# Low parts of six weight granules per layer subtracted on GpSimd instead of VectorE

## The chip, the cores and the metric

The kernel runs on one core of a Trainium2 chip. The core's engines are TensorE (PE in the profile, its weight loads PEld), VectorE (DVE), ScalarE (ACT), GpSimd (POOL) and SyncE (SP, which here only issues DMAs). Each engine works through its own instructions in order, and engines wait for one another by semaphores. The metric is the device time of one execution in microseconds. Before the change the median of three runs is 723.58 us (723.31 to 723.88).

## The reference

The program is a decoder trunk of two layers for 256 tokens of width 1024, in float32. Each layer projects x with w_in into the queries, keys and values of two attention branches and two gates, runs a stick-breaking attention and a block-sparse softmax attention, merges the branches, and adds a SwiGLU part with its own norm:

```python
branch_sb = merge_heads(o_sb) @ w_branch_sb
branch_mb = merge_heads(o_mb) @ w_branch_moba
merged = jax.nn.sigmoid(g_sb) * branch_sb + jax.nn.sigmoid(g_mb) * branch_mb
mix = merged @ w_out
x = layer_norm(DEEPNORM_ALPHA * x + mix, ...)
x = layer_norm(DEEPNORM_ALPHA * x + swiglu(x, w_gate, w_up, w_down), ...)
```

## The kernel before

**Weights.** All weights of a layer come as 122 granules of 128 x 1024 float32 (512 KB each). A product in float32 is made of three matmuls on rounded values (the type fp32r): with a = a_hi + a_lo for both sides, it is hi x hi, hi x lo and lo x hi (`mm3`). So each granule needs two parts. `WeightStream.line` makes them: SP loads the granule into one of six `raw` buffers; ACT casts it to the high part (`whi<-raw`, a ring of ten slots); then DVE subtracts, `wlo = raw - whi` (`wlo<-raw,whi`, a second ring of ten). Both operands of this subtraction lie in SBUF. The load of granule g + 6 waits until granule g has been subtracted, because it reuses its buffer. Seven granules per layer (`SOFT_IN_LAYER`, 22 to 40) take another way: POOL issues two DMAs that cast and accumulate, without DVE.

**The stage that matters here.** Within a layer, granules 40 to 47 are the two branch projections (40 to 43 the stick-breaking one, whose results are called pa, 44 to 47 the MoBA one, pb), and 48 to 55 the output projection (pw), one granule for each 128 rows of w_out. In the profile and in the built program layer 1's granules are 122 higher: 45 is 167 there. While TensorE works on pa, the MoBA heads come to an end (pp and mb_w: the parts of their weights; mb_o: their products; mb_f and mb_turn: their sums; omb_hi and omb_lo: the parts of their result). Then TensorE works on pb, which reads omb. DVE multiplies the gates with pa and pb (each product with one operand in PSUM, where matmuls write), adds the two gates of a chunk (`l0gate<-l0gate`, both operands in one SBUF tile), and ACT and DVE make the parts m_hi and m_lo, which TensorE reads in pw. After pw comes the norm, whose two small steps `ve` run on POOL.

**The order.** The code fixes the order of each engine's instructions while it is built. `Weave` keeps an estimated clock for each engine (`act_t`, `dve_t`, `pool_t`, and `t` for TensorE). Side works such as `line` are generators; after each group of three matmuls `tick` runs those that are due by the estimated clocks. When an estimate changes, instructions change places on all engines. `dve` counts n/960 us and a fixed part for an instruction, `act` n/1200, and `pool` 0.55 us for whatever it is given.

Of the kernel before, what the change touches and what calls it, by code (L numbers as in the profile page):

```python
# [7 lines left out]
F32 = mybir.dt.float32  # L8
# [21 lines left out]
GCOLS = 1024  # L30
NG_LAYER = 122
# [3 lines left out]
class Weave:  # L35
# [18 lines left out]
        self.dve_t = max(self.dve_t, e) + n / 960.0 + DVE_FIXED  # L54
        return self.dve_t + HOP

    def pool(self, e, f, *args, **kw):
        f(*args, **kw)
        self.pool_t = max(self.pool_t, e) + 0.55
        return self.pool_t + HOP  # L60

    def add(self, gen, due=0.0, last=False):
# [36 lines left out]
class WeightStream:  # L99
# [5 lines left out]
    def __init__(self, nc, pool, rings, w, total, weave):  # L105
        self.nc, self.pool, self.rings, self.w, self.total, self.weave = nc, pool, rings, w, total, weave
        self.soft = [g for g in range(total) if SOFT(g)]
        self.hard = [g for g in range(total) if not SOFT(g)]
        self.loaded = self.split = self.cast = self.done = 0
        self.limit = NSPLIT - 1  # L110
        self.current = 0
        self.dma_t = 1.7
        self.raw, self.parts, self.there, self.ready = {}, {}, {}, {}
# [36 lines left out]
    def _part(self, i, g):  # L150


        at = g % NSPLIT * GCOLS + (ON[i] if self._on(g) else 0)
        return self.rings[i][:, at:at + GCOLS]
# [4 lines left out]
    def line(self):  # L159

        nc, weave = self.nc, self.weave
        while self.split < len(self.hard):
            g = self.hard[self.split]
            ahead = g - self.current
            if g > self.limit:
                yield weave.t + 0.1
                continue
            if ahead >= LEAD and max(weave.dve_t, weave.act_t) > weave.t + BACKLOG:
                yield weave.t + 0.2
                continue  # L170
            self.load(self.split + NRAW)
            if ahead > 0:
                yield self.there[g]
            hi, lo = (self._part(i, g) for i in range(2))
            t = self.raw.pop(g)
            e = weave.act(self.there[g], GCOLS, nc.scalar.copy, hi, t)
            if g - self.current > 0:
                yield e
            e = weave.dve(e, GCOLS, nc.vector.tensor_sub, lo, t, hi.bitcast(F32))
            self.parts[g], self.ready[g] = (hi, lo), e  # L180
            self.split += 1
            self.load(self.split + NRAW)
# [36 lines left out]
    def allow(self, g):  # L219

        reaches = self._on(g) and not self._on(g - NSPLIT + 1) and g % NSPLIT < NSPLIT - 1
        self.limit = max(self.limit, min(g - reaches, self.total - 1))
# [25 lines left out]
    return g % NG_LAYER in SOFT_IN_LAYER  # L248


NSPLIT = 10
ON = (16, 48)
STATIONARY = ((8, 20), (24, 50), (64, 100), (130, 140), (146, 170), (186, 220))
# [15 lines left out]
def hybrid_trunk_kernel(ctx: ExitStack, tc: tile.TileContext, w, xT_in, x_in, ln_in,  # L269
# [39 lines left out]
    def turn(e):  # L309

        was = None
        while True:
# [5 lines left out]
            else:  # L318
# [3 lines left out]
        return taken[0] - 1  # L322
    rings = [p.tile([P, NSPLIT * GCOLS + on], F32R, name=n)
             for p, n, on in ((ring0, "whi", ON[0]), (ring1, "wlo", ON[1]))]
# [137 lines left out]
    def both_tokens(name, g0, put):  # L462

        acc = [bankM(f"{name}{t}", [P, WIDTH]) for t in range(2)]
        for t, k in ((0, 0), (0, 1), (0, 2), (1, 0), (1, 1), (0, 3), (1, 2), (1, 3)):
            tok_major(acc[t], g0 + k, t, k == 0, k == 3, 2 * k)
            if t == 1:
                ws.allow(g0 + k + NSPLIT)
            if k == 3:
                put(t, acc[t])  # L470

    def first_projections(names, puts):

        acc = [bankB(n, [P, 2, WIDTH]) for n in names]
        for kc in range(KC):
            for j in range(2):
# [7 lines left out]
                if kc % 2:  # L484
                    ws.allow(g + NSPLIT)
                if kc == KC - 1:
# [245 lines left out]
    def two_pairs(line, name, ps, qks, free, e, sides, *args):  # L732


        while len(turned) < free:
            yield
        e = max(e, *turned[max(free - 2, 0):free], 0.0)
        yield e + MARGIN
        ss = [bankB(f"{name}{p}_s", [P, 2, 512]) for p in ps]
        pe_after(e)  # L740
        e = scores([(s, *qk) for s, qk in zip(ss, qks)])
        for p, s in zip(ps, ss):
            sides.append(weave.add(line(f"{name}{p}", p, s, e, *args)))
# [17 lines left out]
    def norm_line(name, t, junk, gb):  # L761

        x = xs[t]
        st = small.tile([P, 2], F32, tag="st", name=f"{name}_st{t}")
        nmu = small.tile([P, 1], F32, tag="nmu", name=f"{name}_nmu{t}")
        ve = small.tile([P, 1], F32, tag="ve", name=f"{name}_ve{t}")
        e = pe_done()
        for h in range(2):
            e = residual(e, x, halves[h], junk[:, h, :], st[:, h:h + 1])
        e = dve(e, 16, nc.vector.tensor_scalar, nmu, st[:, 0:1], st[:, 1:2], -1.0 / D, op0=OP.add, op1=OP.mult)  # L770
        e2 = act(e, D + 100, nc.scalar.activation, junk, x.rearrange("p (h c) -> p h c", h=2), AF.Square,
                 bias=nmu, accum_out=ve)
        e2 = pool(e2, nc.gpsimd.tensor_scalar, ve, ve, 1.0 / D, EPS, op0=OP.mult, op1=OP.add)
        e2 = pool(e2, nc.gpsimd.tensor_tensor, ve, ve, mhalf, op=OP.pow)
        ends = [e for _, e in scale_shift(e, x, halves, nmu, OP.add, ve, *gb, e2)]
        for h in range(2):
            i = yield from turn(ends[h])
            tp = bankC(f"{name}_tp{t}{h}", [P, 4, P])
            pe_after(ends[h])
            for j in range(4):  # L780
                transpose(tp[:, j, :], x[:, (4 * h + j) * P:(4 * h + j + 1) * P])
            ks = slice(h * 4, (h + 1) * 4)
            ts = slice(t * P, (t + 1) * P)
            e = pe_done()
            yield e
            left[i] = xT_ready[t] = yield from split_line(xT_hi[:, ks, ts], xT_lo[:, ks, ts], tp, 512, e)
# [33 lines left out]
    for l in range(DEPTH):  # L820
# [41 lines left out]
        def sb_pair(p, g):  # L862
            hi, lo = (pl.tile([P, 2, S], F32R, tag=f"qk{n}{p % 2}", name=f"{L}qk{n}{p}", bufs=1)
                      for n, pl in (("hi", work), ("lo", page2 if p % 2 else work)))
            ps = bankM(f"{L}pqk{p}", [P, 2, S])
            feat_major(ps[:, 0, :], g)
            feat_major(ps[:, 1, :], g + 1)
            qks[p] = [(hi[:, i, :], lo[:, i, :]) for i in range(2)]

            def line():  # L870
                ends[p] = yield from split_line(hi, lo, ps, 512, pe_done())
                if p % 2:
                    e = max(ends[p - 1], ends[p])
                    yield e + MARGIN
                    yield from two_pairs(sb_line, f"{L}sb", (p - 1, p), (qks[p - 1], qks[p]),
                                         l * 2 * NPAIR + p - 1, e, sides, v_sb, o_sb, sigmoids, passed)

            sides.append(weave.start(line()))
# [280 lines left out]
```

## Time and profile before

| | us |
|---|---|
| median of three runs | 723.58 |
| the profiled execution, its own time | 723.1 |
| its span, first to last instruction | 721.3 |
| TensorE busy | 710.4 |
| DVE busy | 526.5 |
| ACT busy | 389.7 |
| POOL busy | 34.5 |

The span is what the trace covers; the execution's own time has 1.8 us around it. A row of the timeline reads: start, duration, engine, line, operation, output <- inputs, shapes, count; in brackets the idle time before it and what ended that. Several instructions of one kind in a row are merged (x4), with the whole duration. Buffer numbers are left out there. An instruction's duration is a little longer than its distance to the next, since successive instructions overlap slightly.

### The profile page before, as it was taken

To read this page: it belongs to the slowest core of one execution; us is meant where nothing else is said; L and a number is where in the kernel's file an instruction comes from. 1 tells how busy PE (TensorE), PEld (TensorE's weight loads), DVE (VectorE), ACT (ScalarE), POOL (GpSimd) and SP (SyncE) were. 2 spreads that over 40 slices of the span, in tenths; PEclk is the share of its full clock that TensorE was granted. 3 is DMA by queue.
4 is the path that set the end of the run, shared out by engine and by line. 5 is a ranking of instruction groups with operands and counts; after the bars stand their busy time and mean duration, and the time that the engine had idled before them with its cause. 6 is when DMAs were issued, how large, how long until landed. Compare 5 with 4: busy or idle time off the path is not lost.

```text
span 721.3 us, 12733 instructions
## 1 busy us (share of the span) xinstructions
PE 710.4 (98%) x4992; PEld 651.9 (90%) x4992; DVE 526.5 (73%) x786; ACT 389.7 (54%) x581; POOL 34.5 (5%) x48
## 2 busy tenths in 40 slices
PE   9999999999999999999999999999999999999995
PEld 7889899987899999988889889999888999998885
DVE  5999886798886666644588887869989776665416
ACT  5767667663665554533356566776556555454300
POOL 0001110000000000000000111000010000000001
PEclk9999999999999999999999999999999999999998
DMA  8998889677596656476259579695748965562501
GB/s 287 343 337 238 232 209 267 208 273 239 183 330 224 200 184 202 146 290 205 65 176 354 158 215 233 199 307 177 271 164 290 292 201 184 198 202 93 229 1 59
DMA packets 61597, 156.26 MB, mean 217 GB/s; under 512 B 10720, under 2 KB 21984, under 8 KB 61536
## 3 DMA queue, kind: packets, MB, share of 16 engines
q1 hardware_dynamic: 56848, 140.50, 57.6%
q0 software_dynamic: 4544, 14.68, 9.2%
q8 instruction: 39, 0.64, 0.4%
q10 hardware_dynamic: 144, 0.26, 0.1%
q14 instruction: 22, 0.18, 0.1%
HBM read 148.08 MB, written 7.34 MB: 215 GB/s over the span
## 4 chain that ended last, share of the span: by engine, by line
PE 92%; DVE 3%; DMA 3%; ACT 1%; issue 0%; POOL 0%; SPq 0%; POOLq 0%; DVEq 0%; ACTq 0%
PE l1pf L427 14%; PE l0pf L427 14%; PE l0pd L427 8%; PE l0pg L427 6%; PE l1pg L427 6%; PE l1pe L427 4%; PE l1pd L427 4%; PE l1pqk L427 3%; PE l1pw L427 3%; PE l1pft L427 3%; PE l0pft L427 3%; PE l1pvq L427 3%; PE l0pw L427 2%; DMA raw<-in_w_dram 2%; PE l0pv L427 2%; PE l1pk L427 2%
## 5 line engine op out<-in xcount | busy, mean ns | idle before, releaser
L53 DVE TENSOR_TENSOR wlo<-raw,whi 128x1024 fp32r<-128x1024 f32 (+1 forms) x234 | 277.2, 1202 | 81.2 <-ACT whi L48 78.3
L48 ACT CAST whi<-raw 128x1024 fp32r<-128x1024 f32 (+1 forms) x233 | 237.6, 1036 | 81.7 <-PE l0pd L427 19.6
L427 PE MATMUL l1pf<-xT_hi,wlo 128*128 128x256 f32 x288 | 79.6, 276 | 0.0
L427 PE MATMUL l1pf<-xT_hi,whi 128*128 128x256 f32 x288 | 79.6, 276 | 0.0
L427 PE MATMUL l1pf<-xT_lo,whi 128*128 128x256 f32 x288 | 79.6, 276 | 0.0
L427 PE MATMUL l0pf<-xT_hi,whi 128*128 128x256 f32 x288 | 79.5, 276 | 0.0
L427 PE MATMUL l0pf<-xT_hi,wlo 128*128 128x256 f32 x288 | 79.5, 276 | 0.0
L427 PE MATMUL l0pf<-xT_lo,whi 128*128 128x256 f32 x288 | 79.5, 276 | 0.0
L427 PEld LDWEIGHTS l1pf<-xT_lo,whi 128*128 128x128 f32 x288 | 54.1, 188 | 0.0
L427 PEld LDWEIGHTS l1pf<-xT_hi,whi 128*128 128x128 f32 x288 | 54.1, 188 | 0.0
L427 PEld LDWEIGHTS l1pf<-xT_hi,wlo 128*128 128x128 f32 x288 | 54.1, 188 | 0.0
L427 PEld LDWEIGHTS l0pf<-xT_hi,whi 128*128 128x128 f32 x288 | 54.1, 188 | 0.0
L427 PEld LDWEIGHTS l0pf<-xT_lo,whi 128*128 128x128 f32 x288 | 54.1, 188 | 0.0
L427 PEld LDWEIGHTS l0pf<-xT_hi,wlo 128*128 128x128 f32 x288 | 54.1, 188 | 0.0
L427 PE MATMUL l0pg<-xT_hi,whi 128*128 128x256 f32 x128 | 35.8, 280 | 0.2 <-DVE l0vmb L53 0.2
L427 PE MATMUL l1pg<-xT_hi,whi 128*128 128x256 f32 x128 | 35.7, 279 | 0.0
L427 PE MATMUL l0pg<-xT_hi,wlo 128*128 128x256 f32 x128 | 35.4, 277 | 0.0
L427 PE MATMUL l0pg<-xT_lo,whi 128*128 128x256 f32 x128 | 35.4, 277 | 0.0
L427 PE MATMUL l1pg<-xT_lo,whi 128*128 128x256 f32 x128 | 35.4, 276 | 0.0
L427 PE MATMUL l1pg<-xT_hi,wlo 128*128 128x256 f32 x128 | 35.3, 276 | 0.0
L427 PE MATMUL l0pd<-whi,l0h_hi 128*128 128x512 f32 x88 | 34.5, 392 | 0.0
L427 PE MATMUL l0pd<-whi,l0h_lo 128*128 128x512 f32 x88 | 34.3, 389 | 0.0
(365 smaller groups left out, 1783.9 us busy)
## 6 DMA issues: line engine op xcount, KB each, us to landing
raw<-in_w_dram SPq DMA_DIRECT2D x226, 512.0 KB, 4.7
whi<-in_w_dram POOLq DMA_DIRECT2D x14, 512.0 KB, 5.1
wlo<-in_w_dram POOLq DMA_DIRECT2D x14, 512.0 KB, 6.4
ln<-in_ln_dram SPq DMA_DIRECT2D x8, 512.0 KB, 6.1
raw<-in_w_dram SPq DMA_DIRECT2D x7, 256.0 KB, 5.7
l0mb_scr<-l0mb_turn SPq DMA_DIRECT2D x4, 384.0 KB, 5.0
l0mb_turn<-l0mb_scr SPq DMA_DIRECT2D x16, 96.0 KB, 6.2
l1mb_scr<-l1mb_turn SPq DMA_DIRECT2D x4, 384.0 KB, 7.3
```

Source lines behind the costliest of these rows:

```text
L48: f(*args, **kw)
L53: f(*args, **kw)
L427: nc.tensor.matmul(o, a, b, start=start, stop=stop)
```

## The change

Six granules of each layer, 45, 47, 49, 51, 53 and 55 counted within the layer, get their low part by GpSimd's `tensor_sub` in place of VectorE's. `pool` gets an argument for the time to count, and these six count 2.4 us on POOL's estimated clock. Operands, result and what waits for it are otherwise the same.

```diff
-    def pool(self, e, f, *args, **kw):
+    def pool(self, e, f, *args, took=0.55, **kw):
         f(*args, **kw)
-        self.pool_t = max(self.pool_t, e) + 0.55
+        self.pool_t = max(self.pool_t, e) + took
         return self.pool_t + HOP
...
-            e = weave.dve(e, GCOLS, nc.vector.tensor_sub, lo, t, hi.bitcast(F32))
+            if g % NG_LAYER in POOLED:
+                e = weave.pool(e, nc.gpsimd.tensor_sub, lo, t, hi.bitcast(F32), took=POOL_SUB)
+            else:
+                e = weave.dve(e, GCOLS, nc.vector.tensor_sub, lo, t, hi.bitcast(F32))
...
+POOLED = (45, 47, 49, 51, 53, 55)
+POOL_SUB = 2.4
```

Since the order follows the estimated clocks, other instructions of the stage move as well. On DVE in layer 0, while TensorE works on pa, there stood before (the number behind raw is the granule):

```order
L53 TENSOR_TENSOR wlo_99<-raw45_1442,whi_98 128x1024
L53 TENSOR_TENSOR l0gate1_1129<-l0gate1_1129,l0pa1_1644 128x2x256
L53 TENSOR_TENSOR pp_168<-l0mb2_turn_1375,pp_168 128x768
L53 TENSOR_TENSOR l0omb_lo_1018<-l0mb1_f_1630,l0omb_hi_1017 128x256
L53 TENSOR_TENSOR l0gate2_1310<-l0gate2_1310,l0pa2_1678 128x2x256
L53 TENSOR_TENSOR l0mb3_w1_1704<-l0mb3_turn_1412,l0mb3_w0_1703 128x768
L53 TENSOR_TENSOR wlo_99<-raw46_1477,whi_98 128x1024
```

and now:

```order
L53 TENSOR_TENSOR l0gate1_1129<-l0gate1_1129,l0pa1_1644 128x2x256
L53 TENSOR_TENSOR pp_168<-l0mb2_turn_1375,pp_168 128x768
L53 TENSOR_TENSOR wlo_99<-raw46_1477,whi_98 128x1024
L53 TENSOR_TENSOR l0omb_lo_1018<-l0mb1_f_1630,l0omb_hi_1017 128x256
L53 TENSOR_TENSOR l0mb3_w1_1714<-l0mb3_turn_1412,l0mb3_w0_1713 128x768
L53 TENSOR_TENSOR l0gate2_1310<-l0gate2_1310,l0pa2_1679 128x2x256
L53 TENSOR_TENSOR wlo_99<-raw48_1504,whi_98 128x1024
```

Granule 45 has left DVE, 46 has moved ahead of omb_lo and of mb3_w1 (mb_w in the profile), and the product with pa2 behind it. On TensorE the matmuls that read mb3_w come six matmuls earlier in layer 0 and twelve later in layer 1.

On DVE in layer 0, while TensorE begins pw, before:

```order
L53 TENSOR_TENSOR wlo_99<-raw51_1665,whi_98 128x1024
L53 TENSOR_TENSOR l0gate3_1455<-l0gate3_1455,l0pb3_1768 128x2x256
L53 TENSOR_TENSOR l0m1_lo_1846<-l0gate2_1310,l0m1_hi_1845 128x512
L53 TENSOR_TENSOR l0gate3_1455<-l0gate3_1455 128x2x256
L53 TENSOR_TENSOR wlo_99<-raw52_1729,whi_98 128x1024
L53 TENSOR_TENSOR wlo_99<-raw53_1789,whi_98 128x1024
L53 TENSOR_TENSOR wlo_99<-raw54_1807,whi_98 128x1024
L53 TENSOR_TENSOR wlo_99<-raw55_1824,whi_98 128x1024
L53 TENSOR_TENSOR l0m1_lo_1846<-l0gate3_1455,l0m1_hi_1845 128x512
```

and now:

```order
L53 TENSOR_TENSOR l0gate3_1455<-l0gate3_1455,l0pb3_1778 128x2x256
L53 TENSOR_TENSOR l0m1_lo_1846<-l0gate2_1310,l0m1_hi_1845 128x512
L53 TENSOR_TENSOR l0gate3_1455<-l0gate3_1455 128x2x256
L53 TENSOR_TENSOR wlo_99<-raw54_1756,whi_98 128x1024
L53 TENSOR_TENSOR l0m1_lo_1846<-l0gate3_1455,l0m1_hi_1845 128x512
```

One subtraction of four is left ahead of the last m_lo, that of granule 54; granule 52 stands further up, ahead of the first m_lo.

On POOL in layer 0, between the last weight DMA and the norm, there is now:

```order
L134 DMA wlo_99<-in_w_dram 128x2x512
L58 ISA
L58 TENSOR_TENSOR wlo_99<-raw45_1442,whi_98 128x1024
L58 TENSOR_TENSOR wlo_99<-raw47_1491,whi_98 128x1024
L58 TENSOR_TENSOR wlo_99<-raw49_1540,whi_98 128x1024
L58 TENSOR_TENSOR wlo_99<-raw51_1665,whi_98 128x1024
L58 TENSOR_TENSOR wlo_99<-raw53_1732,whi_98 128x1024
L58 TENSOR_TENSOR wlo_99<-raw55_1817,whi_98 128x1024
L58 TENSOR_SCALAR l0a_ve0_1994<-l0a_ve0_1994 128x1
```

Before, the six subtractions were not there; the row of `ISA` was, in the same place. Layer 1 has the same six, 167 to 177.

## The prediction

> **What bounds the kernel now.** I read the page's busy times first, then the list of TensorE's waits, then the two stretches of the program that the change touches, instruction by instruction.
>
> ```profile
> span 721.3 us, 12733 instructions
> PE 710.4 (98%) x4992; PEld 651.9 (90%) x4992; DVE 526.5 (73%) x786; ACT 389.7 (54%) x581; POOL 34.5 (5%) x48
> PE busy L384 <- DVE mhalf L379: 1.5, 1, 1.5
> PE l0pw L427 <- DVE l0m_lo L53: 0.8, 1, 0.8
> PE l0pw L427 <- DVE wlo L53: 0.7, 1, 0.7
> PE l0pg L427 <- DVE l0vmb L53: 0.2, 1, 0.2
> ```
>
> TensorE is busy for 98% of the span. It waits 3.2 us in all, and the change can reach only the two waits at l0pw, layer 0's output projection. Here they are:
>
> ```profile
> 159.00 0.39 PE L427 MATMUL l0pw<-whi,l0m_hi 128*128 128x512 f32 x1
> 160.10 0.50 PE L427 MATMUL l0pw<-wlo,l0m_hi 128*128 128x512 f32 x1 [0.71 <-DVE wlo L53]
> 160.44 0.39 PE L427 MATMUL l0pw<-whi,l0m_lo 128*128 128x512 f32 x1
> 160.67 0.40 PE L427 MATMUL l0pw<-whi,l0m_hi 128*128 128x512 f32 x1
> 162.95 0.39 PE L427 MATMUL l0pw<-wlo,l0m_hi 128*128 128x512 f32 x1
> 164.10 0.50 PE L427 MATMUL l0pw<-whi,l0m_lo 128*128 128x512 f32 x1 [0.76 <-DVE l0m_lo L53]
> 158.82 4.62 DVE L53 TENSOR_TENSOR wlo<-raw,whi 128x1024 fp32r<-128x1024 f32 x4
> 163.36 0.69 DVE L53 TENSOR_TENSOR l0m_lo<-l0gate,l0m_hi 128x512 fp32r<-128x512 f32 x1
> ```
>
> Undisturbed, these matmuls start 0.23 us apart (160.44 to 160.67). From 159.00 to 160.10 is 0.87 too much, from 162.95 to 164.10 0.92: **1.8 us** are lost. Both times DVE is late. It subtracts granules 52 to 55 in one run of 4.62 us, and the last l0m_lo stands behind that run. Layer 1 has no such wait, but little slack either:
>
> ```profile
> 133.00:166.00 33.00, 31.53 (x226) 28.85 (x225) 31.83 (x47) 19.02 (x27) 0.00 (x0) 1.00 0.68 227
> 487.00:520.00 33.00, 33.00 (x236) 30.37 (x235) 31.77 (x47) 19.67 (x29) 0.00 (x0) 1.00 0.64 216
> 502.72 0.42 DVE L53 TENSOR_TENSOR l1omb_lo<-l1mb_turn,l1omb_hi 128x256 fp32r<-128x256 f32 x1
> 503.30 0.29 PE L427 MATMUL l1pb<-l1omb_lo,whi 128*128 128x256 f32 x1
> ```
>
> The first two rows give, for the stage in each layer, its length and the busy time of PE, weight loads, DVE, ACT and POOL. In 33 us DVE is busy for 31.8, as full as TensorE, and POOL does nothing. The last l1omb_lo ends at 503.14, and its first reader starts at 503.30: 0.16 us to spare. So DVE is the second bound of this stage, and what DVE loses here TensorE soon loses too.
>
> **What is removed and moved.** Per layer six of DVE's subtractions go to POOL. Four in a row take 4.62 us, so one occupies DVE for 1.15; six are 6.9 us per layer, 13.9 in both. All of them lie in the full stage. Nothing else is added: ACT's casts, the loads and the matmuls are the same in number. Loads wait, in order on SP's queue, for the subtraction that frees their raw buffer, six granules back:
>
> ```profile
> 135.41 1.22 DVE L53 TENSOR_TENSOR wlo<-raw,whi 128x1024 fp32r<-128x1024 f32 x1
> 144.38 1.23 DVE L53 TENSOR_TENSOR wlo<-raw,whi 128x1024 fp32r<-128x1024 f32 x1
> 145.63 4.40 SPq L137 DMA_DIRECT2D raw<-in_w_dram  x4
> ```
>
> The first is granule 45's subtraction, the second 47's, and behind it at 145.63 the loads from granule 53 on go out. By the walk below 45 is done at 136.4, 47 at 140.9, so these loads come no later; the one behind granule 49 (done at 149.5 where it was 148.5) feeds granule 55, whose cast comes near 160. On POOL the subtractions stand behind the last weight DMA, issued at 113.81, and ahead of the norm's short steps at 169.64:
>
> ```profile
> 113.81 1.20 POOL L134 DMA_DIRECT2D wlo<-in_w_dram  x1 [8.68 <-ACT wlo L48]
> 169.64 0.74 POOL L58 TENSOR_SCALAR l0a_ve<-l0a_ve 128x1 f32<-128x1 f32 x1 [54.64 <-ACT l0pw L48]
> ```
>
> In between POOL idles 54.64 us, so neither end is in the way.
>
> **The price of one on POOL.** No row shows a wide POOL subtraction. Below, DVE's own 1.15 us bounds it; above, both operands fetched one after the other at DVE's pace and POOL's longest short step on top, 2 x 1.22 + 0.96 = 3.4. I take 2.4, the figure the change itself plans with (POOL_SUB), in the middle of the bounds. [...]
>
> **Does it run beside DVE?** This decides the sign. The rows with both engines at work are the norms:
>
> ```profile
> 169.58 0.75 DVE L53 SCALAR_TENSOR_TENSOR x<-x,l0a_nmu,ln 128x512 f32<-128x512 f32 x1 [1.31 <-ACT l0pw L48]
> 170.25 0.75 DVE L53 SCALAR_TENSOR_TENSOR x<-x,l0a_nmu,ln 128x512 f32<-128x512 f32 x1
> 170.47 0.96 POOL L58 TENSOR_TENSOR l0a_ve<-l0a_ve,mhalf 128x1 f32<-128x1 f32 x1
> 715.53 0.48 DVE L53 SCALAR_TENSOR_TENSOR x<-x,l1b_mv,ln 128x256 f32<-128x256 f32 x1
> 715.92 0.48 DVE L53 SCALAR_TENSOR_TENSOR x<-x,l1b_mv,ln 128x256 f32<-128x256 f32 x1
> 715.77 0.66 POOL L58 TENSOR_TENSOR l1b_ve<-l1b_ve,mhalf 128x1 f32<-128x1 f32 x1
> ```
>
> DVE's instruction reads two operands from SBUF, x and ln. POOL's reads one column. At 170.47 POOL's takes 0.96 and ends at 171.43, 0.43 after DVE's second (171.00). In the last norm DVE's pieces are shorter, and the same POOL step takes 0.66: it ends at 716.43, 0.42 after the DVE piece that was running when it began (716.01). So POOL's end follows DVE's end, not POOL's own work. The TENSOR_SCALAR at 169.64 fits: it ends at 170.38, 0.05 behind DVE's first (170.33). **POOL waits for a DVE instruction that reads two operands from SBUF.** Whether DVE waits for POOL in turn no row can show: POOL reads a single column there, and the DVE piece at 715.92 takes 0.48 like the one before it.
>
> [...]
>
> I take it that DVE waits too, for as long as POOL reads. In the stage nearly all of DVE's work but the products with pa and pb and the sums with mb_o (one operand in PSUM each) reads two SBUF tiles: wlo, pp, omb_lo, mb_w, the sums of two gates, m_lo.
>
> **The sum.** I walk the new order with DVE's and ACT's durations from the rows and 2.4 us per POOL step, POOL getting its turn at the next end of a DVE instruction:
>
> ```profile
> 132.93 1.05 ACT L48 CAST whi<-raw 128x1024 fp32r<-128x1024 f32 x1
> 133.60 1.78 DVE L53 TENSOR_TENSOR l0mb_f<-l0mb_o,l0mb_f 64x256 f32<-64x256 f32 x4
> 139.08 0.95 DVE L53 TENSOR_TENSOR l0mb_w<-l0mb_turn,l0mb_w 128x768 fp32r<-128x768 f32 x1
> 140.96 1.04 PE L427 MATMUL l0mb_o<-l0mb_w,l0vmb 128*128 128x256 f32 x8
> ```
>
> Layer 0. Granule 45 is cast at 133.98; POOL works until 136.4, mostly beside l0mb_f, and holds pp up for 0.4. Granule 47 gets the port when wlo of 46 ends, near 138.5, until 140.9: omb_lo, then mb_w, stand 2.4 us. mb_w then ends near 142.2, and the matmuls that read it, at 140.96 before and six matmuls earlier now, wait 1.9 us. Granule 49 holds the two omb_lo for 2.4, 51 the second of them or the first sum of gates for 2.4, 53 wlo of 54 for 1.7, 55 the last m_lo for 2.4. Together 11.7 us held up, 6.9 freed: DVE ends the stage **4.8 us later**. Layer 1, likewise: 1.0 (pp), 0.7 (mb_w), 2.4 (wlo of 48), 2.4 (wlo of 50, and omb_lo with its 0.16 us behind both), 2.0 (sum of gates), 1.6 (m_lo), together 10.1, less 6.9: **3.2 us later**. The sum is 8.0 us. The freed time is in it, so the old stall of 1.8 is not taken off again.
>
> If DVE goes first whenever both want the port, POOL gets in only at instructions with an operand in PSUM. Walked the same way, TensorE loses 4.1 us in layer 0, less the 1.8 lost before, 2.3; and 2.8 in layer 1, at omb_lo (0.7) and at the m_lo of the first gate (2.1): 5.1. Between 5.1 and 8.0 no row decides; I take the middle, 6.5. The profiled execution took 723.1 us, 1.8 around its span of 721.3: 729.6. The median of the runs, 723.58, is 0.5 above that execution, within the rounding of my walk; I forecast **729.5 us**, 0.8% slower. With POOL's bounds instead of 2.4, 1.15 holds up no more than is freed (0), and 3.4 adds up to 1.0 x 12 = 12 us; both ends are far from two operands read in turn at about DVE's pace (2 x 1.15 = 2.3), so the forecast's own range is 725 to 733.
>
> **The rivals.**
>
> ```profile
> 161.59 0.39 PE L427 MATMUL l0pw<-wlo,l0m_hi 128*128 128x512 f32 x1
> ```
>
> No contention (faster). The row is the first reader of granule 53's low part. If DVE does not wait, three of its subtractions, 51, 53 and 55, 3.4 us, vanish from ahead of the last m_lo, and it ends by 160.6 instead of 164.05, before TensorE wants it; 52 now stands ahead of the gates. Then the 1.8 us are all regained and layer 1 stays: 723.1 - 1.8 = 721.3, 0.25% faster. POOL is in time for that: 53 is cast near 156.9 and done at 159.3, wanted at 161.59 - 0.87 = 160.7; 55 is done at 161.8, wanted 2.8 later than 53, at 163.5. This holds up to 3.7 us per POOL step; beyond, POOL itself is late. For it: POOL is idle, and the DVE piece at 715.92 was not lengthened. Against it: POOL's steps do wait for DVE, so something is shared.
>
> POOL yields (no change). POOL waits for DVE but not the other way round. Then 53, begun at 156.9, meets two-operand DVE work (the sum of gates 3, wlo of 54, m_lo: 0.6 + 1.15 + 0.6) and ends near 161.5, 0.8 late; 55 follows with DVE nearly done, 161.5 + 2.4 = 163.9, in time for 163.5 + 0.8. TensorE loses 0.8 where it lost 1.8: 722.1, within a few tenths of the bound of what can be told. For it: the rows show this direction only. [...]
>
> **How the numbers follow.** Forecast 0.67, no contention 0.17, POOL yields 0.16. A measurement of this kernel tells about 0.2%, 1.4 us, from no change. The forecast's case gives slower 0.65, and 0.02 same; no contention gives faster 0.15 and same 0.02 (its gain is only 0.4 over the bound); POOL yields gives same 0.10, faster 0.04, slower 0.02. Faster 0.19, same 0.14, slower 0.67. The range runs from 722.5, which leaves out the faster case, to 733.
>
> **What would show it.** DVE's two-operand instructions in the two stages would have lengths of 2 to 3.5 us, ending just behind a POOL step; POOL's twelve would take about 2.4 or, where they begin inside a DVE instruction, more. TensorE's waits would stand at mb_w or omb_lo in layer 0, at omb_lo in layer 1, and at the last m_lo, 6 to 10 us in all where there were 1.5. If DVE's wlo still takes 1.22 everywhere, there is no contention and I am wrong in the sign. If DVE is held up as I say but TensorE's waits stay under 3 us, the slack was larger than I read.

## The result, and the profile after

The changed kernel takes 731.22 us (730.95 to 731.7) where the kernel before, run beside it, takes 723.44 (723.02 to 723.88). The ratio is 1.0113, with a 95% interval of 1.0101 to 1.0125: the change costs 7.8 us. The profiled execution took 731.7 us.

From the page of the changed kernel: the span, TensorE's and DVE's busy times, and the row of POOL's subtractions (busy us, mean ns of one | idle before them).

```profile
span 729.9 us, 12743 instructions
PE 713.6 (98%) x4992; PEld 655.6 (90%) x4992; DVE 531.9 (73%) x774; ACT 389.6 (53%) x581; POOL 67.7 (9%) x60
L58 POOL TENSOR_TENSOR wlo<-raw,whi 128x1024 fp32r<-128x1024 f32 x12 | 32.9, 2750 | 71.0 <-ACT whi L48 51.6
```

DVE makes twelve instructions fewer (774 for 786) and is busy 5.4 us longer. The twelve that left it took 13.9 us, so what stayed has grown by some 19 us. TensorE's waits (what it waited for: us in total, times, longest):

```profile
PE l0pb L432 <- DVE l0omb_lo L53: 1.8, 1, 1.8
PE l0pw L432 <- DVE l0m_lo L53: 1.6, 1, 1.6
PE l0mb_o L432 <- DVE l0mb_w L53: 1.3, 1, 1.3
PE l1pb L432 <- ACT l1omb_hi L48: 1.2, 1, 1.2
PE l1pb L432 <- DVE l1omb_lo L53: 0.9, 1, 0.9
```

These are 6.8 us where there were 1.5, beside two others that were there before (1.5 at the start, 0.2 at pg). Where DVE's growth sits, the timeline of layer 0 shows (start, duration, engine, line, operation; x2 is two instructions with their whole duration):

```profile
133.22 1.78 DVE L53 TENSOR_TENSOR l0mb_f<-l0mb_o,l0mb_f 64x256 f32<-64x256 f32 x4
133.69 2.44 POOL L58 TENSOR_TENSOR wlo<-raw,whi 128x1024 fp32r<-128x1024 f32 x1 [19.37 <-DVE l0mb_f L53]
137.43 2.94 POOL L58 TENSOR_TENSOR wlo<-raw,whi 128x1024 fp32r<-128x1024 f32 x1 [1.30 <-ACT whi L48]
138.00 2.64 DVE L53 TENSOR_TENSOR l0omb_lo<-l0mb_f,l0omb_hi 128x256 fp32r<-128x256 f32 x1
146.40 4.94 POOL L58 TENSOR_TENSOR wlo<-raw,whi 128x1024 fp32r<-128x1024 f32 x2 [6.04 <-ACT whi L48]
146.46 5.17 DVE L53 TENSOR_TENSOR l0omb_lo<-l0mb_turn,l0omb_hi 128x256 fp32r<-128x256 f32 x2
162.41 5.88 POOL L58 TENSOR_TENSOR wlo<-raw,whi 128x1024 fp32r<-128x1024 f32 x2 [11.07 <-ACT whi L48]
163.32 2.74 DVE L53 TENSOR_TENSOR wlo<-raw,whi 128x1024 fp32r<-128x1024 f32 x1 [0.61 <-ACT whi L48]
165.98 2.86 DVE L53 TENSOR_TENSOR l0m_lo<-l0gate,l0m_hi 128x512 fp32r<-128x512 f32 x1
```

A row of omb_lo that took 0.42 us in the kernel before takes 2.64, and ends 0.27 us behind the POOL step that began while the instruction ahead of it was running. Two of them take 5.17, beside two POOL steps of 4.94. The last m_lo, 0.69 before, takes 2.86. At the top of the fence the contrast: the four sums l0mb_f have one operand in PSUM, take 1.78 us as before, and the POOL step beside them takes 2.44.

The stage as a whole, in each layer from the same place in TensorE's work (3.5 us behind its last matmul of pg) to the end of the last m_lo: length, then the busy time (and number) of PE, weight loads, DVE, ACT and POOL, and the granted clock. Before:

```profile
132.69:164.05 31.36, 29.94 (x220) 27.56 (x218) 29.89 (x46) 19.30 (x28) 0.00 (x0) 1.00 0.66 223
487.27:516.98 29.71, 29.71 (x220) 27.70 (x219) 28.75 (x45) 18.80 (x28) 0.00 (x0) 1.00 0.63 212
```

And after:

```profile
132.31:168.84 36.53, 31.76 (x220) 29.42 (x218) 33.72 (x40) 19.37 (x28) 16.20 (x6) 0.95 0.62 209
491.93:525.75 33.82, 31.64 (x219) 29.43 (x219) 31.37 (x40) 19.53 (x28) 16.68 (x6) 0.95 0.62 210
```

The stage is 5.2 us longer in layer 0 and 4.1 in layer 1, together 9.3. The span grew by 8.6; the 0.7 between them lies in small shifts outside (this execution came to layer 0's stage 0.4 us earlier, for one). DVE is busy 3.8 and 2.6 us longer, though it has five or six instructions fewer, and idle 1.3 and 1.5 us longer. The last column but two shows something new: the granted clock was 0.95, where it was 1.00.

### The profile page after: what moved, and what is told of

It is laid out like the page before. It is cut to its first block, busy times and chain, and to the rows that moved or that the text cites. A ratio compares the mean times of both kernels' runs of the same rounds, so it can differ in the third digit from the quotient of the medians.

```text
span 729.9 us, 12743 instructions
## 1 busy us (share of the span) xinstructions
PE 713.6 (98%) x4992; PEld 655.6 (90%) x4992; DVE 531.9 (73%) x774; ACT 389.6 (53%) x581; POOL 67.7 (9%) x60
## 4 chain that ended last, share of the span: by engine, by line
PE 77%; DMA 7%; issue 7%; DVE 5%; ACT 1%; POOL 1%; SPq 0%; POOLq 0%; DVEq 0%; ACTq 0%
PE l1pf L432 13%; PE l0pf L432 13%; PE l0pd L432 8%; PE l1pg L432 5%; PE l1pe L432 4%; PE l1pd L432 4%; DMA raw<-in_w_dram 3%; PE l1pqk L432 3%; PE l1pw L432 3%; PE l1pvq L432 3%; PE l0pft L432 3%; PE l1pft L432 3%; DVE wlo L53 2%; PE l0pw L432 2%; PE l0pv L432 2%
## 5 line engine op out<-in xcount | busy, mean ns | idle before, releaser
L53 DVE TENSOR_TENSOR wlo<-raw,whi 128x1024 fp32r<-128x1024 f32 (+1 forms) x222 | 269.2, 1228 | 82.6 <-ACT whi L48 79.9
L58 POOL TENSOR_TENSOR wlo<-raw,whi 128x1024 fp32r<-128x1024 f32 x12 | 32.9, 2750 | 71.0 <-ACT whi L48 51.6
```

## The experiments

All comparisons are with the kernel before, run on the same chip beside each.

**Writing without reading.** POOL gets a memset of the low part in place of the subtraction: the same plan, the same DVE work removed, a POOL instruction at each place of POOL's order, but one that reads nothing. Six granules per layer are then without their low part.

```diff
-                e = weave.pool(e, nc.gpsimd.tensor_sub, lo, t, hi.bitcast(F32), took=POOL_SUB)
+                e = weave.pool(e, nc.gpsimd.memset, lo.bitcast(F32), 0.0, took=POOL_SUB)
```

> The changed kernel, but in each of the twelve places GpSimd only writes the low part (fills it with zero) and reads nothing, so six granules per layer lack their low part. The plan and the order on every engine stay those of the changed kernel. Theory (GpSimd's reading of two SBUF operands shuts VectorE out): nothing is shut out, VectorE's l0omb_lo is back at 0.42 us, the waits at l0pw are gone too because six subtractions have left VectorE, no stretch at half clock: 721 to 722.5 us. Rival 1 (the moved order costs the time): the loss stays, 729 or more. Rival 2 (GpSimd is late, not in the way): between, as the filling may be shorter than 2.4 us; VectorE's own instructions would be no longer in either kernel.

Measured: 720.39 us, ratio 0.9963 [0.9948, 0.9977], a little less than expected. Its group of DVE's subtractions (busy us, mean ns), and one of the places where a memset and a subtraction lie side by side:

```profile
L53 DVE TENSOR_TENSOR wlo<-raw,whi 128x1024 fp32r<-128x1024 f32 x214 | 257.9, 1220 | 81.3 <-ACT whi L48 77.6 <-issue 0.6
151.13 0.96 POOL L58 MEMSET wlo<- 128x1024 f32 x1 [7.25 <-issue]
151.29 1.22 DVE L53 TENSOR_TENSOR wlo<-raw,whi 128x1024 fp32r<-128x1024 f32 x1
```

No DVE subtraction is lengthened (mean 1220 ns, as one takes alone), and no wait of the stage is left. So this POOL instruction, which only writes, does not hold DVE up (1.22 us beside a memset of 0.96). Two reservations: the memset is shorter than the subtraction (0.96 us), and it needs neither the load nor the cast, so that it starts earlier and only some of the twelve lie beside work with two SBUF operands. The time of this run is therefore no measure of what one hold costs.

**The order alone.** The same plan and order, with the subtractions issued to DVE.

```diff
-                e = weave.pool(e, nc.gpsimd.tensor_sub, lo, t, hi.bitcast(F32), took=POOL_SUB)
+                e = weave.pool(e, nc.vector.tensor_sub, lo, t, hi.bitcast(F32), took=POOL_SUB)
```

> The changed kernel's plan and order, but the twelve subtractions are issued to VectorE, at the place where the plan puts them. Theory: no contention is left; VectorE does as much as before the change, in a slightly other order: 722.5 to 726 us, all wlo at 1.22 us. Rival 1 (the order costs the time): 729 or more. Rival 2 (GpSimd late): as the theory, so this run tells the order alone.

Measured: 724.14 us, ratio 1.0015 [1.0005, 1.0024]. From the list of waits:

```profile
PE l1pb L432 <- DVE l1omb_lo L53: 0.8, 1, 0.8
PE l1pb L432 <- ACT l1omb_hi L48: 0.6, 1, 0.6
```

There are 0.3 us more at mb_o in each layer. The order alone costs 1.1 us of the 7.8, and it works in opposite ways in the two layers. The waits at l0pw are gone in layer 0, since the last m_lo stands ahead of the late subtractions; in layer 1 omb comes late. The changed kernel is some 7 us slower than this one, which has the same order: 0.6 us on the average for each of its twelve POOL steps.

**Reading one operand.** POOL copies raw into the low part, which then isn't the remainder.

```diff
-                e = weave.pool(e, nc.gpsimd.tensor_sub, lo, t, hi.bitcast(F32), took=POOL_SUB)
+                e = weave.pool(e, nc.gpsimd.tensor_copy, lo, t, took=POOL_SUB)
```

> The changed kernel with GpSimd copying the raw granule into the low part in place of subtracting: it reads one operand, not two (so the low part of six granules per layer is wrong by the high part). Theory: GpSimd reads half as much and holds VectorE up about half as long, near 1.2 us each, no longer than VectorE's own subtraction would take: 721.5 to 725 us, VectorE's l0omb_lo near 1.5 us where it was 2.64. Rival 1 (order): 729 or more.

Measured: 720.78 us, ratio 0.997 [0.9958, 0.9982], again less than expected. In the timeline of layer 0:

```profile
134.27 1.05 POOL L58 CAST wlo<-raw 128x1024 fp32r<-128x1024 f32 x1 [3.61 <-DVE l0mb_f L53]
137.66 1.76 POOL L58 CAST wlo<-raw 128x1024 fp32r<-128x1024 f32 x1 [2.35 <-DMA raw<-in_w_dram]
138.44 1.26 DVE L53 TENSOR_TENSOR l0omb_lo<-l0mb_f,l0omb_hi 128x256 fp32r<-128x256 f32 x1
```

The copy takes 1.05 us beside the sums with a PSUM operand. Where it meets two-operand work it is held (1.76), and holds omb_lo: 1.26 instead of 0.42. So the lock is there with one operand too. The copy is hardly longer than the memset (1.05 us for 0.96), which lengthened nothing: the reading holds DVE up, not the length of POOL's instruction. The hold lasts until POOL's instruction ends (at 139.42, and omb_lo 0.28 us behind it), and at one this short TensorE hardly waits (0.2 us). The copy is also ready earlier, since it needs no cast, so this run does not price the length alone.

**Another place.** Six granules of the SwiGLU's weights (70 to 90) instead.

```diff
-POOLED = (45, 47, 49, 51, 53, 55)
+POOLED = (70, 74, 78, 82, 86, 90)
```

> Six other granules per layer on GpSimd: 70, 74, 78, 82, 86 and 90, in the feed-forward part, where VectorE has idle time (it waits some 35 us there for ScalarE and TensorE). Theory: VectorE's instructions that meet a GpSimd step grow by up to 2.4 us there as well, but ten slots of lead hide it and TensorE does not wait: 723 to 724.2 us, no worse and no better than before the change. Rival 2 (GpSimd's results are late): waits of TensorE at l0pf and l1pf, over 725 us.

Measured: 723.6 us, ratio 1.0008 [0.9999, 1.0018]. DVE's tile wlo with the shortest, median and longest duration in ns:

```profile
L53 DVE TENSOR_TENSOR wlo<-raw,whi x222: 685/1224/3472, 4.7 to 688.1; 128x1024 fp32r<-128x1024 f32 x107, 128x512 fp32r<-128x512 f32 x4
```

DVE is held up here too (up to 3.47 us for a subtraction), but TensorE does not wait where it uses these weights, and the time stays. So here the hold costs nothing, where DVE has slack. Nor is anything gained, since DVE's freed time was not wanted there.

**Fewer steps.** Four kernels share out the twelve.

```diff
-            if g % NG_LAYER in POOLED:
+            if g in POOLED:
```

> The change in layer 0 alone (granules 45 to 55; layer 1 as before). Theory (the loss is made in each layer by itself: TensorE's waits for DVE instructions held up by POOL, plus one stretch of half clock behind the longest wait): layer 0 alone loses 3.5 us net in waits and 1.7 us to the clock, 5.2 in all: 727.5 to 728.5 us where before takes 723.0, with one stretch of half clock near 153, none in layer 1, and layer 1's waits as before. Rival (the two stretches of half clock are there for another reason than the waits, such as a power limit on the whole run): both or neither appear, and the time is 726 to 727 or 729 to 730.

Measured: 727.54 us, ratio 1.0065 [1.0051, 1.0079]. Layer 0 alone costs 4.4 of the 7.8 us. The stretch of half clock that was expected near 153 was not there; in the profiled execution, which took 729.42 us, one began at 169.30, behind another wait (below).

```diff
-POOLED = (45, 47, 49, 51, 53, 55)
+POOLED = (45, 47, 49)
```

> Only granules 45, 47 and 49 of each layer on POOL. Theory: the waits at mb_o (1.4 us) and at the omb parts (2.0 in layer 0, 2.5 in layer 1) stay, with the half clock behind them if they reach about 2.1 us; the last m_lo has the DVE run of 51 to 55 before it again, so the 1.8 at l0pw stay too. 727 to 731 us, POOL steps 2.4 to 2.9 each. Rival (the loss comes from the late three, which shift DVE as a whole): 723 to 725.

Measured: 727.15 us, ratio 1.0057 [1.0044, 1.0071], 4.0 us slower, with waits at most of the places named:

```profile
PE l0mb_o L432 <- DVE l0mb_w L53: 1.3, 1, 1.3
PE l1pb L432 <- ACT l1omb_hi L48: 1.2, 1, 1.2
PE l0pw L432 <- DVE l0m_lo L53: 0.9, 1, 0.9
PE l1pb L432 <- DVE l1omb_lo L53: 0.8, 1, 0.8
```

The wait of 2.0 us at the omb parts of layer 0 did not come, and of the 1.8 at l0pw only 0.9 stayed. The 2.1 us of the expectation is an estimate: in the changed kernel starts of TensorE's matmuls 2.12 us apart at l0pb (149.56 and 151.68) were followed by half clock, and starts 2.03 apart at l0pw (166.87 and 168.90) were not.

```diff
-POOLED = (45, 47, 49, 51, 53, 55)
+POOLED = (51, 53, 55)
```

> Only granules 51, 53 and 55 of each layer on POOL. Theory: no POOL step meets omb_lo or mb_w in layer 0, so no wait at mb_o or l0pb and no half clock; at l0pw the last m_lo is held up by about 2 us instead of standing behind a run of subtractions, which cancels: 722.5 to 724.5 us. Rival (any three POOL steps cost half of the change's loss): 726.5 to 727.5.

Measured: 730.86 us, ratio 1.011 [1.0095, 1.0126]. This was a clear miss: the late three alone cost as much as all six. From its waits and its timeline:

```profile
PE l0pw L432 <- DVE wlo L53: 3.2, 2, 2.2
PE l1pw L432 <- DVE l1m_lo L53: 1.4, 1, 1.4
PE l0pw L432 <- POOL wlo L58: 0.6, 1, 0.6
```

```profile
160.18 5.53 POOL L58 TENSOR_TENSOR wlo<-raw,whi 128x1024 fp32r<-128x1024 f32 x2 [5.61 <-ACT whi L48]
160.65 2.82 DVE L53 TENSOR_TENSOR l0m_lo<-l0gate,l0m_hi 128x512 fp32r<-128x512 f32 x1
163.39 5.66 DVE L53 TENSOR_TENSOR wlo<-raw,whi 128x1024 fp32r<-128x1024 f32 x3
```

The expectation went by the last m_lo alone. In this kernel's order subtractions that TensorE wants soon stand behind it, and they are held up with it: three in 5.66 us. One low part also came late from POOL itself (0.6 us), and TensorE's clock was halved once, from 168.01. All that could have been the order's doing, so the same order was run with all subtractions on DVE:

```diff
-                e = weave.pool(e, nc.gpsimd.tensor_sub, lo, t, hi.bitcast(F32), took=POOL_SUB)
+                e = weave.pool(e, nc.vector.tensor_sub, lo, t, hi.bitcast(F32), took=POOL_SUB)
```

> The kernel with 51, 53 and 55 on POOL, its order and plan kept, but the six subtractions of both layers issued to VectorE. Theory (what that kernel lost, 4.6 us by the end of layer 0's output projection and 3.2 in layer 1, is DVE held up by POOL's three reads): without POOL's reads 722 to 725 us. Rival (its order is the cause: the plan places the subtractions of granules 52 and 54 late, so that TensorE waits for them): most of the loss stays, 728 to 731, with waits for wlo at l0pw.

Measured: 722.27 us, ratio 0.9989 [0.998, 0.9998]. The order was not to blame. The 8.6 us between the two kernels come with the six POOL steps that read, 1.4 us each, POOL's own lateness and the half clock included. The costs do not add up over the steps: all twelve cost 7 us by the same comparison.

```diff
-POOLED = (45, 47, 49, 51, 53, 55)
+POOLED = (45,)
```

> Granule 45 of each layer alone on POOL. Theory: in layer 0 its POOL step lies beside DVE's sums l0mb_f with one operand in PSUM, which it does not lengthen, so 1.15 us of DVE are freed for at most 0.5 held up (pp), in layer 1 it holds pp up by 1.0; TensorE's waits stay where they were: 722.5 to 723.5 us, ratio 0.999 to 1.001. Rival (each POOL step costs a twelfth of the loss, 0.65 us): 724.3.

Measured: 723.02 us, ratio 0.9999 [0.999, 1.0008]. The time stays, but the two layers differ. In layer 0 the POOL step lies beside the sums with an operand in PSUM and lengthens only pp, by 0.1 us; the waits at l0pw fall from 1.5 us to 0.6. In layer 1 it meets pp, which took 0.95 before:

```profile
489.32 1.91 DVE L53 TENSOR_TENSOR pp<-l1mb_turn,pp 128x768 fp32r<-128x768 f32 x1
```

TensorE then waits 0.7 us at l1pb, where it waited for nothing before. So a step beside PSUM work holds up next to nothing and can gain, and the other step takes that back. How much of either is the changed order was not tested.

**In four pieces.** Each POOL subtraction made in four of 256 columns, the order elsewhere kept.

```diff
-                e = weave.pool(e, nc.gpsimd.tensor_sub, lo, t, hi.bitcast(F32), took=POOL_SUB)
+                for j in range(4):
+                    q = slice(256 * j, 256 * j + 256)
+                    e = weave.pool(e, nc.gpsimd.tensor_sub, lo[:, q], t[:, q], hi[:, q].bitcast(F32), took=POOL_SUB / 4) - HOP
+                e += HOP
```

> The changed kernel with each of the POOL subtractions made in four pieces of 256 columns, the order on all other engines kept. Theory (POOL holds DVE's two-operand instructions out for as long as one POOL instruction reads, and DVE gets in between two of them): a piece takes about 0.65 us, DVE's instructions beside it are lengthened by at most about 0.7 us each, omb_lo ends 1 to 2 us earlier than in the changed kernel; DVE loses as much over the stage, but later and in more places: 726 to 730 us. Rival (DVE stays shut out for the four pieces in a row): lengths of 2 to 3 us as in the changed kernel and 731 to 733.

Measured: 726.89 us, ratio 1.0051 [1.0034, 1.0068]. In the timeline, and in the list of waits:

```profile
134.13 2.86 POOL L58 TENSOR_TENSOR wlo<-raw,whi 128x256 fp32r<-128x256 f32 x4 [20.08 <-DVE l0mb_f L53]
145.76 8.34 POOL L58 TENSOR_TENSOR wlo<-raw,whi 128x256 fp32r<-128x256 f32 x8 [1.85 <-ACT whi L48]
145.82 1.85 DVE L53 TENSOR_TENSOR l0omb_lo<-l0mb_turn,l0omb_hi 128x256 fp32r<-128x256 f32 x2
```

```profile
PE l0pw L435 <- POOL wlo L58: 1.8, 1, 1.8
```

The two omb_lo take 1.85 us instead of 5.17, and the waits at mb_o and pb are gone. DVE and POOL take turns: four pieces take 2.86 us beside PSUM work, 0.72 each, and eight take 8.34 here, while DVE runs eight instructions (145.82 to 153.51). DVE's instructions with two operands in SBUF grow by up to about 0.55 us beside the pieces (pp 1.50 for 0.95, wlo 1.76 for 1.22), less than one piece. POOL itself is now late, and TensorE waits 1.8 us for one of its low parts. So the grain of the lock is one instruction, and the cut into pieces halves the loss (3.9 us for 7.8) without removing it.

**The half clock.** In the changed kernel TensorE's clock was halved twice. The windows of its trace (length, PE busy, granted clock, DMA share, GB/s) ahead of each halving and behind it:

```profile
149.68:153.09 3.41, 1.56 (x14) 1.00 0.46 154
153.09:156.50 3.41, 3.41 (x18) 0.50 0.80 214
508.08:511.49 3.41, 1.32 (x8) 1.00 0.91 277
511.49:514.90 3.41, 3.41 (x18) 0.50 0.62 177
```

Twice TensorE ran at half speed for 3.41 us, which is 1.7 us of work lost each time, 3.4 in all: a term that the prediction did not have. On TensorE's own account the 8.6 us of the span are 5.3 more of waiting and 3.2 more of busy time. To see what it is worth, matmuls by a zero weight were put into TensorE's queue in the places where it waits, so that it never idles for long. They add zeros and wait for nothing.

```diff
+    def fill(o, a, n):
+        for _ in range(n):
+            nc.tensor.matmul(o[:64], nil, a, start=False, stop=False)
...
+FILL_B = ((0, 16, 0), (11, 10, 0))
+FILL_W = 7
```

> The changed kernel, with matmuls by a zero weight put into TensorE's queue where it waited: 16 of 256 columns ahead of the reader of the last l0omb_lo (1.8 us), 11 and 10 around the waits for the last l1omb parts (1.25 and 1.1 us), 7 of 512 ahead of the last l0m_lo (1.6 us). They add zeros to the sum and wait for nothing; all else is as in the changed kernel. Theory (TensorE's clock is halved for the 3.41 us behind a 3.41 us stretch in which it idled for more than about half): no stretch of half clock is left, DVE is held up as before, and the two stretches' 3.4 us go: 727 to 729 us, where the changed kernel takes 731.2. Rival (the half clock comes from elsewhere, or is a mere reflection of waits): 730.5 to 732, or more by what the added matmuls cost.

Measured: 731.31 us, ratio 1.0116 [1.0102, 1.0129], so no change from the changed kernel's 731.22: the expectation was wrong. The half clock did go, with no stretch of it left in the trace. But the time did not come back. TensorE's work on layer 1's pb and pw in the changed kernel, and then with the filling (duration in ns min/median/max, first and last start):

```profile
L432 PE MATMUL l1pb<-l1omb_hi,wlo x32: 276/276/415, 501.4 to 517.2; 128*128 128x256 f32 x32
L432 PE MATMUL l1pw<-whi,l1m_lo x32: 387/389/398, 517.8 to 539.9; 128*128 128x512 f32 x32
```

```profile
L436 PE MATMUL l1pb<-l1omb_hi,wlo x32: 276/276/282, 500.5 to 514.7; 128*128 128x256 f32 x32
L436 PE MATMUL l1pw<-whi,l1m_lo x32: 389/389/504, 515.3 to 539.0; 128*128 128x512 f32 x32
```

And from the list of waits with the filling:

```profile
PE l1pw L436 <- DVE l1m_lo L53: 0.8, 1, 0.8
```

With the filling, layer 1's pb begins 0.9 us earlier, a gain of layer 0, and ends 2.5 us earlier, 1.6 gained by the full clock. But pw ends only 0.9 earlier (539.0 for 539.9): TensorE now waits for DVE's m_lo, 0.8 us in one place and less in others. In layer 1 all of the 1.6 is given back within the stage, because TensorE had been slow only while DVE was late anyway. In layer 0 the trace keeps 0.8 of the 1.7 (pw's last matmul starts at 182.1 instead of 182.9), and the medians do not show even that. So at most about 1 us of the loss is the half clock's; the rest of the 3.4 turns into waiting when the clock is full.

**A version that beats both.** The order of the plan was good in layer 0 and bad in layer 1, and POOL's reading was bad in both. So: the plan's order in layer 0 alone, with the subtractions on DVE.

```diff
-            if g % NG_LAYER in POOLED:
-                e = weave.pool(e, nc.gpsimd.tensor_sub, lo, t, hi.bitcast(F32), took=POOL_SUB)
+            if g in POOLED:
+                e = weave.pool(e, nc.vector.tensor_sub, lo, t, hi.bitcast(F32), took=POOL_SUB)
```

> The changed kernel's order in layer 0 alone, with the six subtractions of layer 0 left on VectorE; layer 1 as before. Theory (in layer 0 the order alone puts the last m_lo ahead of the late subtractions, and no POOL step holds DVE up): the 1.8 us at l0pw go and nothing comes in their place, but for 0.3 to 0.6 at mb_o: 721.3 to 722.3 us where before takes 723.0. Rival (order makes no difference to TensorE in the sum): 722.7 to 723.5.

Measured: 721.46 us, ratio 0.9979 [0.997, 0.9988], 1.6 us faster than the kernel before. All of TensorE's waits but the two (at the start and at pg) that the kernel before has outside the stage too:

```profile
PE l0mb_o L432 <- DVE pp L53: 0.3, 1, 0.3
```

The 1.5 us of waits at l0pw are gone without a single instruction moved to another engine.

## Why the prediction was right, and where it was off

The forecast was 729.5 us and slower; it came out 731.2 and slower, inside the forecast's own range of 725 to 733.

- **Contention.** Right, and both ways, as assumed without a row for it. DVE's two-operand instructions have lengths of 2.6 to 2.9 us and end just behind a POOL step. The runs with a memset and with a copy, almost equally long, show that the reading is the cause. In the traces 0.42 became 2.64 beside the subtraction, 1.26 beside the copy, and 1.22 stayed 1.22 beside the memset. The walk and the sum speak of a port that both engines want and that is free beside work with an operand in PSUM. No run shows a port; what the runs show in its place is turns, an omb_lo that ends 0.27 us behind the POOL step, and sums with a PSUM operand that keep their 1.78 us beside a POOL step of 2.44.
- **The price of a POOL step.** 2.4 us was taken; 2.44 was measured where nothing is in its way.
- **The places.** Three were named in layer 0: mb_w at 1.9 us (1.3 measured), omb_lo (1.8) and the last m_lo (1.6). In layer 1 omb_lo was named (0.9), but its first part, omb_hi from ACT, comes late as well (1.2): the sums that it is made from stand behind two subtractions that took 4.57 us, where two alone take 2.35. The order alone already makes 0.6 of this wait. The sum was to be 6 to 10 us of waits, and 6.8 stand there.
- **The step that failed is the middle.** Between 8.0 us (POOL first) and 5.1 (DVE first) I took 6.5, because no row decided. The trace of after decides for POOL: the step at 137.43 was issued while DVE's wlo was running and got its turn at that instruction's end, ahead of the omb_lo that DVE had next. The walk for that case gave 4.8 and 3.2 us; the stage was 5.2 and 4.1 us longer. With 8.0 the forecast would have been 731.1. That this lies so near is partly luck, by the next two points.
- **Inside the sum, two errors cancel.** The held-up time was put at 11.7 and 10.1 us. By the lengthened rows it was 10.4 in layer 0 (0.1 at pp, 2.2 at omb_lo, 4.4 at the next two, 1.5 at wlo, 2.2 at the last m_lo), and by the same reading 8.0 in layer 1. But the 6.9 us freed per layer did not all count against it: DVE idled 1.3 and 1.5 us more inside the stage, waiting for TensorE and ACT. Most of these waits (0.61 in layer 0; 0.47, 0.35 and 0.69 in layer 1) stand in the kernel with the memset too (0.60; 1.11, 0.36 and 0.69), where nothing is held up: with six subtractions gone DVE comes to the next instruction before its input is there. The walk had let DVE run through. Nor had it the half clock, of which little counted.
- **The order's own effect was not priced.** That it costs 1.1 us by itself, and that it helps in layer 0 and hurts in layer 1, came out only in the runs of the order alone. The 1.8 us at l0pw that the rival without contention counted on were the order's to gain: they come back with no work moved at all.
- **The rivals.** Both fall: no contention, by the lengthened rows; that POOL yields, by omb_lo, which waits for POOL.

## What to carry to other kernels

Before work goes from VectorE to an idle GpSimd, look at the operands of what VectorE does beside it. In these runs, where VectorE read two operands from SBUF and GpSimd read one or two, they took turns instruction by instruction (0.42 us became 1.26 beside one operand and 2.64 beside two), and a GpSimd step of 2.4 us that freed 1.15 made VectorE later where it had no slack. Against the same order with all subtractions on VectorE, a step cost 0.6 us on the average of the twelve, 1.4 where only the late three of a layer were moved, and nothing where VectorE had slack; beside PSUM work it held up next to nothing (0.1 us at pp). When a change moves both the work and the order, run the order by itself first, since it may hold the whole gain.

## What was not expected of the hardware

**Half clock came in stretches of 3.41 us that fit one grid, each behind a stretch in which TensorE idled for a little over half or more.** The two stretches of half clock in the changed kernel begin 358.40 us apart (153.09 and 511.49), 105 times the 3.413 that each lasts in the trace; the half clock at the kernel's end begins 215.04 us behind the second (726.53), 63 times 3.413. Taking that grid in the other traces, from the half clock at the end of each, every stretch of half clock within a kernel follows one in which TensorE was busy for 1.58 us or less, as here in the kernel with POOL's steps in four pieces:

```profile
162.04:165.45 3.41, 1.58 (x7) 1.00 0.10 25
165.45:168.86 3.41, 3.28 (x9) 0.50 0.74 282
```

and none follows one with 1.76 us or more, as in the kernel with 45, 47 and 49:

```profile
503.03:506.44 3.41, 1.76 (x14) 1.00 0.76 261
506.44:509.85 3.41, 3.10 (x27) 1.00 0.77 270
```

So the boundary lies between 1.58 and 1.76 of 3.41, about half, as far as the profile's modelled ends of matmuls tell. Whether a wait was followed by half clock depended here on where the grid fell: the wait of 1.8 us at l0pb was followed by it in the changed kernel, and the same wait of 1.8 us in the kernel with layer 0 alone was not, where it lay across two stretches with TensorE busy for 1.97 and 3.01 us.

**A loss of speed can be nearly free.** 3.4 us of TensorE's work were lost to the half clock and at most about 1 us of it shows in the time, because just behind TensorE would have waited for VectorE's lateness instead.
